# Two output projections of a hybrid trunk: keep token chunks where they first land instead of loading them again for the forms

## The chip, the cores and the metric

The kernel runs on one core of a Trainium2 chip. The metric is the device time of one execution in microseconds, as a median of several runs. The core has five engines with instruction streams of their own: TensorE (PE, with its weight loads shown apart as PEld), VectorE (DVE), ScalarE (ACT), GpSimd (POOL) and SyncE (SP). An engine works through its instructions in order; a wait at one of them holds all behind it. SyncE issues nearly all transfers between DRAM and the on-chip memory (SBUF).

## The reference, cut to what matters

Two layers on 512 latent and 128 context tokens of width 2048, in fp32. Each layer normalizes and modulates its input, projects it, runs four kinds of mixers over the columns, concatenates their gated outputs and sends them through one output projection with a gated residual:

```python
def even_mixer(h, w_in, w_out, ...):
    qa, ka, va, ga, ub, bb, cb, gb = split_cols(h @ w_in, EVEN_SPLIT)
    ...
    y_a = merge_heads(o) * jax.nn.silu(ga)
    y_b = gated_short_conv(ub, bb, cb, conv_w) * jax.nn.silu(gb)
    return jnp.concatenate([y_a, y_b], axis=-1) @ w_out, new
...
        xp = xp + gt_p * out_p
        xs = xs + gt_s * out_s
```

The odd layer's mixers are others; its last line, `jnp.concatenate([y_c, y_d], axis=-1) @ w_out`, has the same shape: (640 tokens x 2048) times (2048 x 2048). The change lies in these two products alone.

## The kernel before

The mixer's output lies in DRAM as 16 chunks `ydram[0..15]` (`yd0` to `yd15` below). Chunk k holds rows 128k to 128k + 127 of the contracted dimension, each with all 640 tokens: 128 x 640 fp32, 320 KB. fp32 products are made of three matmuls: `split` (L226 to L228) writes x as a high part (ScalarE, L227) and the rest as a low part (VectorE, L228), and `proj_q` (L263 to L265) multiplies high by high, high by low and low by high. A split chunk is `hk`, a split weight tile is `wh` and `wl`. Tokens are handled in two halves of 320 columns.

`project` computes the 16 output columns (of 128 each) in three stages:

1. `run_tiles` makes columns 0 to 2 together, over four units. A unit is a quarter of the chunks, in the order 0-3, 8-11, 4-7, 12-15; it has 3 columns x 4 chunks x 2 halves x 3 = 72 matmuls of 128x320. Before a unit, three weight tiles (`raw`, 256 KB, loaded by L240) are split, and the maker (`y0_maker`, `y1_maker`) loads and splits the unit's four chunks.
2. Column 3 alone: 96 matmuls.
3. `run_pairs`: six pairs of columns, with a Winograd-like scheme of seven products per pair. Its weights are `w8` tiles of 8 x 128 rows (A11, A21, A12; 512 KB, L519) and sums of them (L543, L546, L548). Its moving operands are halves of h and five combinations of token halves, the forms.

`forms` is a generator that makes form j from chunks j and j + 8 for j = 0 to 7, in `make_form`: three chained VectorE sums into `sx` (L1173, L1174, L1175), a difference (L1176), and the split of `sx` into T0 to T7 (ScalarE, then VectorE). The differences of forms 0 to 3 go into `room`, which lies in a tile shown as `tables`, those of 4 to 6 into `sf`, and that of form 7 over its own input. Later `project` splits the eight differences over one half of h0 to h7.

Every chunk is loaded twice. First for h: chunks 0 to 3 by the earlier maker (layer 0: L939; layer 1 chunks 0-3 and 8-11: L1726), the others by `late_yin` into the three `xr` buffers (L1217). Then again for the forms, into `w8` buffers (L1189), of which there are four: a form's two are loaded one form ahead. `w8` also takes the pairs' weights.

The order of the instructions on each engine is laid down when the program is built, by a scheduler that looks at which instruction is ready; the generators in `attn`, `forms` among them, are advanced once per column and unit. T4 to T7, `sf`, `xr`, `w8` and `sx` are buffers in one pool per projection (`lay_out`); T4 to T7 are each 7680 bytes wide per partition, three chunks' worth, and empty until their form is made. The residual inputs (L1207, `xr` too) and the sums into them (L1212) end each column.

Of the kernel before, what the change touches and what calls it, by code (L numbers as in the profile page):

```python
# [11 lines left out]
F32 = mybir.dt.float32  # L12
F32R = mybir.dt.float32r
# [7 lines left out]
P = 128  # L21
# [4 lines left out]
NT = NS + NP  # L26
HALF = NT // 2
# [23 lines left out]
def trunk_kernel(ctx: ExitStack, tc: tile.TileContext, I: dict, O: dict):  # L51
    nc = tc.nc
# [173 lines left out]
    def split(hi, lo, x):  # L226
        A.activation(hi, x, AF.Copy)  # L227
        V.tensor_sub(lo, x, hi)  # L228
# [24 lines left out]
    HV = ((0, slice(0, HALF)), (1, slice(HALF, NT)))  # L253
# [45 lines left out]
    prep, attn, early = [], [], []  # L299
# [17 lines left out]
    def drain(queue):  # L317
        while queue:
            advance(queue, 1)
# [598 lines left out]
    ydram = [dram.tile([P, NT], F32, name=f"yd{k}") for k in range(KT)]  # L918
# [215 lines left out]
    for i in range(4):  # L1134
        kv, h = i // 2, 2 * i
# [25 lines left out]
    room = [tables[:, i * HALF:(i + 1) * HALF] for i in range(4)]  # L1161
    W_OUT = [I["ev_w_out"][0], I["od_w_out"][0]]
    T, t1 = [], []
    HX = (1, 0)

    def big(tag, shape=(P, NT), dtype=F32, bufs=1):

        n = 6 * HALF if tag[0] == "T" else 8 * P
        return pools["cur"].tile([P, n], dtype, tag=tag, name=tag, bufs=bufs)

    def make_form(x, d, b11, b12, b21, b22, t):
        x2, x3, x4 = (x[:, i * HALF:(i + 1) * HALF] for i in range(3))
        V.tensor_sub(x3, b22, b12)  # L1173
        V.scalar_tensor_tensor(out=x2, in0=x3, scalar=-1.0, in1=b11, op0=ALU.mult, op1=ALU.subtract)  # L1174
        V.scalar_tensor_tensor(out=x4, in0=x2, scalar=-1.0, in1=b21, op0=ALU.mult, op1=ALU.subtract)  # L1175
        V.tensor_sub(d, b11, b12)  # L1176
        t = t.rearrange("p (s n) -> p s n", s=2)
        split(t[:, 0, :], t[:, 1, :], x)
        T.append(t)
        t1.append(d)  # L1180

    def forms():

        f = None

        def load(j):
            ts = [big("w8", bufs=4)[:, 0:NT] for _ in range(2)]
            for i in range(2):
                nc.sync.dma_start(ts[i], ydram[j + 8 * i])  # L1189
            return ts  # L1190

        T.clear()
        t1.clear()
        nxt = load(0)
        for j in range(8):
            (ya, yb), nxt = nxt, (load(j + 1) if j < 7 else None)
            b11, b12, b21, b22 = (t[:, HV[h][1]] for t in (ya, yb) for h in HX)
            x = big("sx")[:, 0:3 * HALF]
            if f is None:
                f = big("sf")  # L1200
            d = room[j] if j < 4 else f[:, (j - 4) * HALF:(j - 3) * HALF] if j < 7 else b11
            make_form(x, d, b11, b12, b21, b22, big(f"T{j}", dtype=F32R))
            yield

    def res_load(l, n):
# [7 lines left out]
                                   in1=xr[:, dsl], op0=ALU.mult, op1=ALU.add)  # L1213

    def late_yin(k):
        t = pools["cur"].tile([P, NT], F32, tag="xr", name="yin", bufs=3)
        nc.sync.dma_start(t, ydram[k])  # L1217
        split(*new_h(k), t)

    def half_of(k0, i):  # L1220
# [90 lines left out]
    def mid_tile(n):  # L1311
        return pools["cur"].tile([P, NT], F32, tag=n, name=n, bufs=1)

    def y0_maker(k):
        if k < 4:
            return make_y0(k)
        if k == 8:
            close("even")
            open_pool("mid")
            lay_out("T7 T6 T5 T4 sf xr w8 sx")  # L1320
            st["acc"], st["sq"] = (mid_tile(n) for n in ("acc", "sq"))
            attn.append(forms())
        late_yin(k)

    def squares(n, sl=slice(0, NT)):
# [364 lines left out]
    for n in range(1, 4):  # L1690
        h = heads[n]
        load, vgen = c_then(n)
# [5 lines left out]
    for n in range(4):  # L1698
# [3 lines left out]
        if n % 2 == 0:  # L1702
            load, vgen = v_then(P, I["cache_d_v"][0, 0, kv], (8 + kv,), O["new_d_v"][0, 0, kv], dense_then(n))
# [11 lines left out]
    def y1_maker(k):  # L1715
        if k == 4:
            drain(attn)
            close("odd")
            open_pool("fin")
            lay_out("T7 T6 xr T5 w8 sx sf T4")  # L1720
            attn.append(forms())
        if k % 8 >= 4:
            late_yin(k)
        else:
            t = pools["cur"].tile([P, 768], F32, tag="P", name="yin", bufs=P_BUFS)[:, 0:NT]
            nc.sync.dma_start(t, ydram[k])  # L1726
            split(*new_h(k), t)
# [82 lines left out]
```

## Time and profile before

| what | value |
|---|---|
| runs of before | 2281.57, 2284.30, 2286.61 us; median 2284.3 |
| profiled execution | 2283.16 us, its span 2281.4 us |
| TensorE busy | 2250.0 us (99%); weight loads 2175.0 (95%) |
| VectorE busy | 1602.0 us (70%) |
| ScalarE busy | 1087.4 us (48%) |
| output projection of layer 0 | from about 914 us, pairs from 976 us |
| output projection of layer 1 | from 2058 us, pairs from 2120 us |
| TensorE's granted clock | 1.00 in all stretches read |

A busy share is an average over stages. Successive matmuls of one kind start every 0.147 us here although each is shown with about 0.31 us, since they overlap; so a short stall need not show as idle time. In the rows, `L263 PE MATMUL pa<-h,wh` is the instruction of line 263 that reads tiles `h` and `wh` and writes `pa`; `yin<-yd` is a transfer from a chunk in DRAM into the tile `yin`; "A <- B: x, n, m" in the list of waits says that A waited for B x us in all, n times, at most m at once. In the table of stretches, a row gives the stretch, its length, then busy time and instructions of PE, PEld, DVE, ACT and POOL, the granted clock, the mean share of the 16 DMA engines that was busy, and GB/s.

### The profile page before, as it was taken

How to read it: one execution, taken by the hardware profiler on the slowest of the kernel's cores; microseconds unless marked ns; L12 is line 12 of the kernel's file. 1: busy time of each engine (PE TensorE's matmuls, PEld its weight loads, DVE VectorE, ACT ScalarE, POOL GpSimd, SP SyncE). 2: the span in 40 equal slices, each digit the busy share in tenths (PEclk: the TensorE clock that was granted, in tenths of full speed). 3: DMA queues.
4: the chain of work that ended last, by engine and by line, in shares of the span. 5: the costliest groups of instructions: out<-in, count | busy, mean ns of one | idle time of the engine just before them, and what ended most of it. 6: DMA issues, size and time to landing. Idle time of an engine off the chain costs nothing.

```text
span 2281.4 us, 41068 instructions
## 1 busy us (share of the span) xinstructions
PE 2250.0 (99%) x15941; PEld 2175.0 (95%) x15941; DVE 1602.0 (70%) x2830; ACT 1087.4 (48%) x2281; POOL 162.5 (7%) x226
## 2 busy tenths in 40 slices
PE   7999999999999999999999999999999999999999
PEld 5889999999999999999999999999999999999999
DVE  5666969779779777788697666565666655557765
ACT  5224535244352222444474444465565676754443
POOL 1001000010000000000100001111111100000101
PEclk9999999999999999999999999999999999999999
DMA  9975645655537564865453333523223212238642
GB/s 324 317 224 174 178 151 167 184 160 173 177 116 239 176 188 147 261 178 147 156 171 113 107 114 110 151 68 104 81 66 98 71 58 62 70 106 268 181 136 62
DMA packets 385395, 344.20 MB, mean 151 GB/s; under 512 B 16418, under 2 KB 342528, under 8 KB 384688
## 3 DMA queue, kind: packets, MB, share of 16 engines
q1 hardware_dynamic: 370624, 296.66, 43.7%
q0 software_dynamic: 13856, 42.76, 5.4%
q8 instruction: 125, 2.05, 0.4%
q10 hardware_dynamic: 720, 2.16, 0.3%
q14 instruction: 70, 0.57, 0.1%
HBM read 301.93 MB, written 39.59 MB: 150 GB/s over the span
## 4 chain that ended last, share of the span: by engine, by line
PE 86%; DMA 4%; issue 4%; DVE 3%; ACT 2%; POOL 0%; SPq 0%; POOLq 0%; DVEq 0%; ACTq 0%
PE pq L606 7%; PE pq L605 7%; PE pq L604 7%; PE pa L263 6%; PE pa L264 6%; PE pb L264 6%; PE pa L265 6%; PE pb L263 6%; PE pb L265 6%; PE pa L277 3%; PE pb L278 2%; PE pb L277 2%; PE pb L279 2%; PE pa L279 2%; PE pa L278 2%
## 5 line engine op out<-in xcount | busy, mean ns | idle before, releaser
L227 ACT ACTIVATE wh<-raw 128x512 fp32r<-128x512 f32 x418 | 263.5, 630 | 543.5 <-PE pb L264 384.4
L228 DVE TENSOR_TENSOR wl<-raw,wh 128x512 fp32r<-128x512 f32 x418 | 287.2, 688 | 201.8 <-ACT wh L227 193.5
L263 PE MATMUL pa<-h,wh 128*128 128x320 f32 x978 | 310.3, 318 | 4.2 <-ACT h L227 2.5
L264 PE MATMUL pa<-h,wh 128*128 128x320 f32 x978 | 304.3, 312 | 2.1 <-DVE h L228 2.1
L265 PE MATMUL pa<-h,wl 128*128 128x320 f32 x978 | 302.8, 310 | 0.0
L264 PE MATMUL pb<-h,wh 128*128 128x320 f32 x978 | 302.5, 309 | 0.0
L265 PE MATMUL pb<-h,wl 128*128 128x320 f32 x978 | 302.4, 309 | 0.0
L263 PE MATMUL pb<-h,wh 128*128 128x320 f32 x978 | 301.6, 309 | 0.7 <-ACT h L1420 0.7
L205 DVE SCALAR_TENSOR_TENSOR acc<-adaw,sT,acc 128x1024 f32<-128x1024 f32 x240 | 299.9, 1276 | 0.0
L604 PE MATMUL pq<-h,wh 128*128 128x320 f32 x672 | 208.7, 311 | 1.4 <-ACT wh L227 1.4
L606 PE MATMUL pq<-h,wl 128*128 128x320 f32 x672 | 207.9, 309 | 0.5 <-DVE wl L228 0.5
L605 PE MATMUL pq<-h,wh 128*128 128x320 f32 x672 | 207.7, 309 | 0.0
L263 PEld LDWEIGHTS pa<-h,wh 128*128 128x128 f32 x978 | 183.6, 188 | 18.1 <-issue 9.3
L264 PEld LDWEIGHTS pa<-h,wh 128*128 128x128 f32 x978 | 183.9, 188 | 8.7 <-DVE h L228 4.6
L263 PEld LDWEIGHTS pb<-h,wh 128*128 128x128 f32 x978 | 183.3, 188 | 1.4 <-ACT h L1420 0.9
L264 PEld LDWEIGHTS pb<-h,wh 128*128 128x128 f32 x978 | 183.6, 188 | 0.9 <-issue 0.8
L265 PEld LDWEIGHTS pa<-h,wl 128*128 128x128 f32 x978 | 183.7, 188 | 0.4 <-issue 0.4
L265 PEld LDWEIGHTS pb<-h,wl 128*128 128x128 f32 x978 | 183.6, 188 | 0.0
L606 PE MATMUL pq<-T,wl 128*128 128x320 f32 x504 | 155.1, 308 | 0.2 <-DVE wl L228 0.2
L604 PE MATMUL pq<-T,wh 128*128 128x320 f32 x504 | 155.1, 308 | 0.1
L605 PE MATMUL pq<-T,wh 128*128 128x320 f32 x504 | 155.2, 308 | 0.0
L277 PE MATMUL pa<-h,wh 128*128 128x320 f32 x448 | 146.5, 327 | 0.0
(482 smaller groups left out, 5410.6 us busy)
## 6 DMA issues: line engine op xcount, KB each, us to landing
adaw<-in_ada_w SPq DMA_DIRECT2D x128, 512.0 KB, 4.1
raw<-in_ev_w_in SPq DMA_DIRECT2D x176, 256.0 KB, 3.4
raw<-in_od_w_in SPq DMA_DIRECT2D x154, 256.0 KB, 2.9
ada<-in_ada_w SPq DMA_DIRECT2D x32, 1024.0 KB, 9.6
w<-in_od_w_in SPq DMA_DIRECT2D x27, 512.0 KB, 3.9
yd<-y POOLq DMA_DIRECT2D x32, 320.0 KB, 3.6
yin<-yd SPq DMA_DIRECT2D x32, 320.0 KB, 4.8
w<-yd SPq DMA_DIRECT2D x32, 320.0 KB, 4.4
```

The lines of the kernel that those rows point to most:

```text
L205: V.scalar_tensor_tensor(out=acc[c], in0=w, scalar=sT[:, kt, c:c + 1], in1=acc[c], op0=ALU.mult, op1=ALU.add)
L227: A.activation(hi, x, AF.Copy)
L228: V.tensor_sub(lo, x, hi)
L263: PE.matmul(ps, wh[:, i, :], hi[:, sl], start=(j == js[0] if alone else (pos == 0 and j == 0)), stop=False)
L264: PE.matmul(ps, wh[:, i, :], lo[:, sl], start=False, stop=False)
L265: last_mm[j % 4] = PE.matmul(ps, wl[:, i, :], hi[:, sl], start=False, stop=(j == js[1] - 1 if alone else (pos == 3 and j == 3)))
L277: PE.matmul(ps, wh[:, j, :], hi[:, sl], start=(qd == 0 and j == 0), stop=False)
L278: PE.matmul(ps, wh[:, j, :], lo[:, sl], start=False, stop=False)
L279: PE.matmul(ps, wl[:, j, :], hi[:, sl], start=False, stop=(qd == 3 and j == 3))
L604: PE.matmul(ps, wh[:, j, :], hi, start=(new and h == 0 and j == 0), stop=False, **kw)
L605: PE.matmul(ps, wh[:, j, :], lo, start=False, stop=False, **kw)
L606: PE.matmul(ps, wl[:, j, :], hi, start=False, stop=(h == 1 and j == 3), **kw)
```

## The change

A chunk that is needed for a form stays where it first lands, so that the form reads it there:

- Layer 0: chunks 8 to 11 are loaded into the four `w8` buffers and both split for h and read by forms 0 to 3; chunks 0 to 3 are still loaded by the forms, now into the `xr` buffers. Chunks 4 to 7 and 12 to 15 go into parts of T5, T6 and T7 (`LATE_AT`), whose own forms come later. 12 of the 32 loads go.
- Layer 1: chunks 4 to 7 and 12 to 15 go into T5 to T7 as well; forms 0 to 3 still load both of their chunks into `w8`. 8 of the 32 loads go.
- `forms` takes the layer, and yields until the chunk j + 8 is there. A form's T is taken only after its sums are in the program, because T6 and T7 hold inputs of forms 6 and 7. Form 7's difference goes into a `w8` buffer of its own.

The arithmetic is unchanged, and so are the numbers of instructions on TensorE, VectorE and ScalarE.

```diff
-        t = t.rearrange("p (s n) -> p s n", s=2)
+        t = (t() if callable(t) else t).rearrange("p (s n) -> p s n", s=2)
...
-    def forms():
-
-        f = None
+    ys, late_t = {}, {}
+    LATE_AT = {4: (5, 0), 12: (5, 1), 5: (6, 0), 13: (6, 1), 14: (6, 2), 6: (7, 0), 7: (7, 1), 15: (7, 2)}
+
+    def y_load(k, t):
+        nc.sync.dma_start(t, ydram[k])
+        return t
+
+    def forms(l):
 
         def load(j):
-            ts = [big("w8", bufs=4)[:, 0:NT] for _ in range(2)]
-            for i in range(2):
-                nc.sync.dma_start(ts[i], ydram[j + 8 * i])
-            return ts
+            if j > 3:
+                return None
+            if l == 0:
+                t = pools["cur"].tile([P, NT], F32, tag="xr", name="yin", bufs=3)
+                return y_load(j, t), None
+            return [y_load(j + 8 * i, big("w8", bufs=4)[:, 0:NT]) for i in range(2)]
...
         for j in range(8):
-            (ya, yb), nxt = nxt, (load(j + 1) if j < 7 else None)
-            b11, b12, b21, b22 = (t[:, HV[h][1]] for t in (ya, yb) for h in HX)
+            cur, nxt = nxt, load(j + 1)
+            while (l == 0 or j > 3) and j + 8 not in ys:
+                yield
+            ya, yb = cur or (ys[j], None)
+            b11, b12, b21, b22 = (t[:, HV[h][1]] for t in (ya, ys[j + 8] if yb is None else yb) for h in HX)
             x = big("sx")[:, 0:3 * HALF]
-            if f is None:
-                f = big("sf")
-            d = room[j] if j < 4 else f[:, (j - 4) * HALF:(j - 3) * HALF] if j < 7 else b11
-            make_form(x, d, b11, b12, b21, b22, big(f"T{j}", dtype=F32R))
+            d = room[j] if j < 4 else f[:, (j - 4) * HALF:(j - 3) * HALF] if j < 7 else big("w8", bufs=4)[:, 0:HALF]
+            make_form(x, d, b11, b12, b21, b22, lambda: big(f"T{j}", dtype=F32R))
             yield
...
     def late_yin(k):
-        t = pools["cur"].tile([P, NT], F32, tag="xr", name="yin", bufs=3)
-        nc.sync.dma_start(t, ydram[k])
+        if k in LATE_AT:
+            g, i = LATE_AT[k]
+            if g not in late_t:
+                late_t[g] = big(f"T{g}")
+            t = late_t[g][:, i * NT:(i + 1) * NT]
+        else:
+            t = big("w8", bufs=4)[:, 0:NT]
+        ys[k] = y_load(k, t)
         split(*new_h(k), t)
...
-            attn.append(forms())
+            attn.append(forms(0))
...
+            ys.clear()
+            late_t.clear()
+            attn.append(forms(1))
```

How this moves the transfers and VectorE's work is seen in three places. In the rows below, a name is followed by its buffer's number; the chunk is the one behind the arrow. The first place is SyncE's queue at the start of layer 0's projection, right behind nine weight loads (`raw`) that are the same in both kernels. Before, the loads for h (`yin`) and those for the forms (`w8`) alternate:

```order
L1217 DMA yin_10570<-yd8_157 128x640
L1217 DMA yin_10575<-yd9_158 128x640
L1217 DMA yin_10580<-yd10_159 128x640
L1189 DMA w8_10614<-yd0_149 128x640
L1189 DMA w8_10615<-yd8_157 128x640
L1217 DMA yin_10585<-yd11_160 128x640
L1189 DMA w8_10618<-yd1_150 128x640
L1189 DMA w8_10619<-yd9_158 128x640
L1217 DMA yin_10721<-yd4_153 128x640
L1189 DMA w8_10655<-yd2_151 128x640
L1189 DMA w8_10656<-yd10_159 128x640
L1217 DMA yin_10726<-yd5_154 128x640
```

In the changed kernel each chunk comes once, and `yin` are now the form's chunks 0 to 3:

```order
L1186 DMA w8_10570<-yd8_157 128x640
L1186 DMA w8_10575<-yd9_158 128x640
L1186 DMA w8_10580<-yd10_159 128x640
L1186 DMA w8_10585<-yd11_160 128x640
L1186 DMA yin_10615<-yd0_149 128x640
L1186 DMA yin_10617<-yd1_150 128x640
L1186 DMA yin_10651<-yd2_151 128x640
L1186 DMA T5_10713<-yd4_153 128x640
L1186 DMA T6_10718<-yd5_154 128x640
L1186 DMA yin_10685<-yd3_152 128x640
L1186 DMA T7_10723<-yd6_155 128x640
L1186 DMA T7_10723<-yd7_156 128x640
```

Behind chunk 8, chunk 11 moves from the 6th to the 4th place, chunk 7 from the 16th to the 12th and chunk 15 from the 27th to the 19th. The load of chunk 3 (the third row from the end) needs a free `xr` buffer, and so waits for VectorE's form 0; chunks 6, 7 and 12 to 15 stand behind it.

The second place is the same queue further on, where column 3 and the first pair are prepared. Before, the first pair's A11 and A21 (L519) come behind form 7's two chunks:

```order
L1189 DMA w8_10911<-yd7_156 128x640
L1189 DMA w8_10912<-yd15_164 128x640
L240 DMA raw_11151<-in_ev_w_out 128x4x128
L240 DMA raw_11153<-in_ev_w_out 128x4x128
L240 DMA raw_11393<-in_ev_w_out 128x4x128
L240 DMA raw_11395<-in_ev_w_out 128x4x128
L1207 DMA xr_11140<-x0d0_165 128x640
L519 DMA w8_11145<-in_ev_w_out 128x8x128
L519 DMA w8_11147<-in_ev_w_out 128x8x128
L1207 DMA xr_11203<-x0d1_166 128x640
```

In the changed kernel they come behind the weights of column 3 (`raw_10942` to `raw_10948`) and the residual inputs (L1216 there):

```order
L240 DMA raw_10942<-in_ev_w_out 128x4x128
L1216 DMA xr_10962<-x0d0_165 128x640
L240 DMA raw_10944<-in_ev_w_out 128x4x128
L1216 DMA xr_10996<-x0d0_165 128x640
L240 DMA raw_10946<-in_ev_w_out 128x4x128
L240 DMA raw_10948<-in_ev_w_out 128x4x128
L1216 DMA xr_11016<-x0d0_165 128x640
L240 DMA raw_11123<-in_ev_w_out 128x4x128
L240 DMA raw_11125<-in_ev_w_out 128x4x128
L519 DMA w8_11117<-in_ev_w_out 128x8x128
L519 DMA w8_11119<-in_ev_w_out 128x8x128
```

The pair's weights wait for `w8` buffers, which the forms 0 to 3 set free there, and no longer for forms 6 and 7.

The third place is VectorE before the first pair of layer 1. N5's weights are L543's sum. Before:

```order
L1174 SCALAR_TENSOR_TENSOR sx_24352<-sx_24352,w8_24322 128x320
L228 TENSOR_TENSOR wl_24522<-w8_24511,wh_24521 128x512
L1175 SCALAR_TENSOR_TENSOR sx_24352<-sx_24352,w8_24323 128x320
L1176 TENSOR_TENSOR w8_24322<-w8_24322 128x320
L228 TENSOR_TENSOR wl_24526<-w8_24511,wh_24525 128x512
L548 TENSOR_TENSOR sf_24571<-w8_24511,w8_24513 128x1024
L228 TENSOR_TENSOR T7_24353<-sx_24352,T7_24353 128x960
L228 TENSOR_TENSOR h7_24035<-w8_24322,h7_24035 128x320
L1212 SCALAR_TENSOR_TENSOR xr_24506<-pb_24335,hgt1_140,xr_24506 128x192
L1212 SCALAR_TENSOR_TENSOR xr_24506<-pb_24335,hgt1_140,xr_24506 128x128
L543 TENSOR_TENSOR sx_24529<-w8_24513,raw_24517 128x512
```

In the changed kernel:

```order
L228 TENSOR_TENSOR wl_24474<-w8_24463,wh_24473 128x512
L228 TENSOR_TENSOR T6_24282<-sx_24277,T6_24282 128x960
L548 TENSOR_TENSOR sf_24523<-w8_24463,w8_24465 128x1024
L1173 TENSOR_TENSOR sx_24303<-T7_24000 128x320
L228 TENSOR_TENSOR wl_24478<-w8_24463,wh_24477 128x512
L1174 SCALAR_TENSOR_TENSOR sx_24303<-sx_24303,T7_24000 128x320
L1175 SCALAR_TENSOR_TENSOR sx_24303<-sx_24303,T7_24000 128x320
L1221 SCALAR_TENSOR_TENSOR xr_24458<-pb_24286,hgt1_140,xr_24458 128x192
L1221 SCALAR_TENSOR_TENSOR xr_24458<-pb_24286,hgt1_140,xr_24458 128x128
L228 TENSOR_TENSOR T7_24309<-sx_24303,T7_24309 128x960
L543 TENSOR_TENSOR sx_24481<-w8_24465,raw_24469 128x512
```

The sum A11 + A21 (L548) now stands ahead of form 7, and the difference L1176 is gone from this place; L543 still comes behind form 7's split.

More of the change, by code (lines that the diff above doesn't have):

```diff
@@ L1180, in make_form @@
         t1.append(d)
-    def forms():
-        f = None
-        def load(j):
-            ts = [big("w8", bufs=4)[:, 0:NT] for _ in range(2)]
-            for i in range(2):
-                nc.sync.dma_start(ts[i], ydram[j + 8 * i])
-            return ts
+    ys, late_t = {}, {}
[4 more added lines that the diff above has]
+    def forms(l):
+        def load(j):
+            if j > 3:
[4 more added lines that the diff above has]
+            return [y_load(j + 8 * i, big("w8", bufs=4)[:, 0:NT]) for i in range(2)]
         T.clear()
         t1.clear()
+        f = big("sf")
         nxt = load(0)
         for j in range(8):
-            (ya, yb), nxt = nxt, (load(j + 1) if j < 7 else None)
-            b11, b12, b21, b22 = (t[:, HV[h][1]] for t in (ya, yb) for h in HX)
+            cur, nxt = nxt, load(j + 1)
[3 more added lines that the diff above has]
+            b11, b12, b21, b22 = (t[:, HV[h][1]] for t in (ya, ys[j + 8] if yb is None else yb) for h in HX)
             x = big("sx")[:, 0:3 * HALF]
-            if f is None:
-                f = big("sf")
-            d = room[j] if j < 4 else f[:, (j - 4) * HALF:(j - 3) * HALF] if j < 7 else b11
-            make_form(x, d, b11, b12, b21, b22, big(f"T{j}", dtype=F32R))
+            d = room[j] if j < 4 else f[:, (j - 4) * HALF:(j - 3) * HALF] if j < 7 else big("w8", bufs=4)[:, 0:HALF]
+            make_form(x, d, b11, b12, b21, b22, lambda: big(f"T{j}", dtype=F32R))
             yield
@@ L1720, in y1_maker @@
             lay_out("T7 T6 xr T5 w8 sx sf T4")
-            attn.append(forms())
+            ys.clear()
+            late_t.clear()
+            attn.append(forms(1))
         if k % 8 >= 4:
```

## The prediction

> **What bounds the kernel now.** I read the page first, for the engine that carries the span and the chain behind it.
>
> ```profile
> span 2281.4 us, 41068 instructions
> PE 2250.0 (99%) x15941; PEld 2175.0 (95%) x15941; DVE 1602.0 (70%) x2830; ACT 1087.4 (48%) x2281; POOL 162.5 (7%) x226
> PE 86%; DMA 4%; issue 4%; DVE 3%; ACT 2%; POOL 0%; SPq 0%; POOLq 0%; DVEq 0%; ACTq 0%
> yin<-yd SPq DMA_DIRECT2D x32, 320.0 KB, 4.8
> w<-yd SPq DMA_DIRECT2D x32, 320.0 KB, 4.4
> ```
>
> TensorE bounds the kernel, and no matmul is added or taken away. So the change is worth only time that TensorE loses in the two output projections, waiting for something that the token loads delay. The last two rows are the 64 loads of the branch outputs: 32 for the moving operand h, 32 for the forms. The change takes 20 of the second kind.
>
> Next I cut each projection at its own boundaries (first matmul of each unit), in the table of busy time by stretches. A unit is one quarter of the tokens' depth under three output columns, 72 matmuls. Layer 0, units 1 to 4, then the single fourth column, then the first 14 us of the pairs:
>
> ```profile
> core 0: us, PE busy (x) PEld busy (x) DVE busy (x) ACT busy (x) POOL busy (x), PEclk, DMA share, GB/s
> 914.29:924.85 10.56, 10.56 (x75) 10.56 (x73) 4.12 (x6) 2.96 (x5) 0.54 (x1) 1.00 0.58 177
> 924.85:937.81 12.96, 11.37 (x75) 10.62 (x73) 10.64 (x18) 7.21 (x11) 0.00 (x0) 1.00 0.84 281
> 937.81:949.22 11.41, 11.09 (x74) 10.56 (x73) 9.59 (x17) 5.93 (x10) 0.00 (x0) 1.00 0.89 274
> 949.22:962.01 12.79, 11.78 (x74) 10.50 (x73) 10.60 (x19) 5.67 (x8) 0.00 (x0) 1.00 0.96 306
> 962.01:976.17 14.16, 14.16 (x97) 14.16 (x97) 14.11 (x30) 8.57 (x16) 1.62 (x3) 1.00 0.89 275
> 976.17:990.25 14.08, 13.31 (x86) 12.32 (x85) 12.55 (x20) 6.50 (x12) 0.54 (x1) 1.00 0.85 246
> ```
>
> Unit 1 runs undisturbed in 10.56 us. Units 2, 3 and 4 take 12.96, 11.41 and 12.79: 2.40, 0.85 and 2.23 us lost. The DMA engines are 84 to 96% busy there. The same for layer 1, from unit 2 on:
>
> ```profile
> 2068.95:2082.15 13.20, 11.62 (x75) 10.61 (x73) 9.14 (x14) 6.75 (x11) 0.00 (x0) 1.00 0.73 231
> 2082.15:2092.71 10.56, 10.56 (x75) 10.56 (x73) 9.15 (x17) 5.24 (x9) 0.00 (x0) 1.00 0.95 312
> 2092.71:2104.10 11.39, 11.24 (x74) 10.56 (x73) 10.04 (x19) 4.58 (x7) 0.00 (x0) 1.00 0.99 315
> 2104.10:2119.74 15.64, 15.64 (x113) 15.62 (x112) 15.04 (x33) 9.09 (x18) 2.59 (x4) 1.00 0.92 282
> 2119.74:2134.00 14.26, 12.78 (x88) 12.23 (x87) 11.95 (x18) 7.60 (x17) 2.58 (x4) 1.00 0.85 250
> ```
>
> Losses of 2.64 (unit 2) and 0.83 (unit 4), and 14.26 - 12.23 = 2.03 after the pairs begin. I measure a loss against the weight loads (PEld), because the matmul busy column hides half: in unit 4 of layer 0 it leaves 12.79 - 11.78 = 1.01, the weight loads leave 2.29, and the length against unit 1 says 2.23. [...]
>
> What TensorE waits for there: the chain of waits of 920 to 990 us, and ScalarE's and SyncE's waits.
>
> ```profile
> 924.81 5.02 DMA yin<-yd
> 936.96 3.73 DMA yin<-yd
> 949.53 3.65 DMA yin<-yd
> 969.80 7.54 DMA w<-in_ev_w_out
> ACT h L227 <- DMA yin<-yd: 11.0, 6, 2.7
> SPq L1189 <- DVE sx L1174: 15.4, 6, 4.5
> ```
>
> The loads of h11, h7 and h15 are on the chain (landing 929.8, 940.7, 953.2), then the pair's first weights. ScalarE waits 11.0 us for token loads. SyncE stands 15.4 us in front of form loads (L1189), waiting for VectorE to free a w8 buffer, and every later load queues behind it. So both traffic and queue order make the h loads late.
>
> **The change part by part.**
>
> The stream of loads. Layer 0: 12 loads of 320 KB go. At the 306 GB/s of unit 4's row one takes 327.68 / 306 = 1.07 us, so 12.8 us of full DMA go. Counted in SyncE's order from y8, y11 was 6th and is 4th, y7 was 16th and is 12th, y15 was 27th and is 19th. That is 2.1, 4.3 and 8.6 us earlier at most: 927.7, 936.4 and 944.6.
>
> Unit 2, layer 0. The first wait there is for h9:
>
> ```profile
> 925.14 0.31 PE L265 MATMUL pa<-h,wl 128*128 128x320 f32 x1
> 926.42 0.41 PE L263 MATMUL pa<-h,wh 128*128 128x320 f32 x1 [0.97 <-ACT h L227]
> 927.28 0.41 PE L264 MATMUL pa<-h,wh 128*128 128x320 f32 x1 [0.45 <-DVE h L228]
> 927.53 0.31 PE L265 MATMUL pa<-h,wl 128*128 128x320 f32 x1
> ```
>
> Three steps of 0.147 us (10.56 / 72) take 2.39 us, so 1.95 of the 2.40 are h9's. y8, y9 and y10 keep their places behind the same nine weight loads, so this stays. The other 0.45 us is h11's, and goes: +0.45 (0 to 0.45).
>
> Unit 3: y7 by 936.4 lands before unit 3 begins (937.4 then). I take 0.75 of 0.85 (0.3 to 0.85).
>
> Unit 4: y15 has over 8 us in hand, and y12 to y14 come just before it. I take 2.1 of 2.23 (1.5 to 2.23).
>
> Start of the pairs, layer 0. The first pair's weights (A11, A21) were loaded into w8 behind the last form loads, at 969.80 by the chain. They now wait for form 3 only, and stand directly behind the fourth column's weights. The wait at the first weights' low part is
>
> ```profile
> 976.32 0.31 PE L605 MATMUL pq<-h,wh 128*128 128x320 f32 x1
> 977.12 0.42 PE L606 MATMUL pq<-h,wl 128*128 128x320 f32 x1 [0.49 <-DVE wl L228]
> ```
>
> and I take 0.6 for it (0 to 0.75: 976.32 would have been followed after 0.147).
>
> VectorE's cover. Every form keeps its instructions: three sums, the difference, and the split.
>
> ```profile
> L228 DVE TENSOR_TENSOR h<-yin,h 128x640 fp32r<-128x640 f32 x12 | 9.8, 821 | 3.7 <-ACT h L227 3.6
> L228 DVE TENSOR_TENSOR T<-sx,T 128x960 fp32r<-128x960 f32 x8 | 9.2, 1155 | 0.7 <-ACT T L227 0.5
> L1174 DVE SCALAR_TENSOR_TENSOR sx<-sx,w 128x320 f32<-128x320 f32 x8 | 3.9, 484 | 0.0
> L227 ACT ACTIVATE T<-sx 128x960 fp32r<-128x960 f32 x8 | 8.0, 1000 | 3.0 <-DVE sx L1175 3.0
> ```
>
> A form is 4 x 0.484 + 1.155 = 3.09 us of VectorE. From 924.85 to 976.17 VectorE is busy 10.64 + 9.59 + 10.60 + 14.11 = 44.94 of 51.32 us, so 6.38 are idle, and none of it in the fourth column. TensorE would come 0.45 + 0.75 + 2.1 + 0.6 = 3.9 us earlier, and VectorE must come as much earlier. Unit 2's 2.32 us of idle I count as lost (the data is not there), which leaves 4.06 for 3.9. That fits only if nearly every gap closes, so I take off 0.4 for lag (0 to 3.9). Layer 0: 3.5 us.
>
> Small things. Forms 6 and 7 now write T6 and T7 only after their difference (L1176) has read the tokens lying there: 0.48 us each before ScalarE's 1.00 us. VectorE has h splits and residual sums to do meanwhile; uncovered it is at most 1.0 us, and I count it in the lag. SyncE issues 20 fewer transfers, which no row of the chain shows as a bound (SPq 0%): nothing. The later allocation and the new w8 buffer for form 7's difference add no instruction; that buffer is free once form 3 has read it: nothing.
>
> Layer 1. Units 2's 2.64 us stay: its h9 to h11 come by L1726 before the change's part begins. In unit 4, y12 to y14 come a few places earlier, but y15 stands behind y3 and y11, which wait for form 1: +0.7 (0 to 0.83). The larger part is N5's weights, in the chain and the timeline:
>
> ```profile
> 2113.58 6.73 DMA w<-in_od_w_out
> 2120.33 1.23 DVE sf L548
> 2123.61 0.61 DVE sx L543
> ```
>
> ```profile
> 2123.20 0.31 PE L606 MATMUL pq<-h,wl 128*128 128x320 f32 x1
> 2124.93 0.41 PE L604 MATMUL pq<-h,wh 128*128 128x320 f32 x1 [1.42 <-ACT wh L227]
> ```
>
> A21's load starts only at 2113.58, when form 7 has let its w8 buffer go; VectorE stands for it, then has L548, the form's split, and only then L543, at which N5 hangs. TensorE's step from 2123.20 to 2124.93 loses 1.58, and 2.03 are lost in all. With A21 waiting for form 3 alone it lands well before. VectorE must then be 2.8 us early with 1.41 + 1.35 + 0.60 = 3.36 us idle in units 3, 4 and the column. I take 1.6 (0.5 to 2.0). Layer 1: 2.3 us.
>
> Sum: 3.5 + 2.3 = 5.8 us. The profiled execution took 2283.16 us, 1.1 below the median of 2284.3; it becomes 2277.4, and the median 2278.5.
>
> **The rivals.**
>
> A. VectorE takes the gain. In the fourth columns it is busy 14.11 of 14.16 and 15.04 of 15.64 us, so what it has not done before goes straight to the pairs' start. If its gaps in units 2 to 4 stay, about one form more (3.09 us) falls into each column: 3.5 - 3.1 and 2.3 - 3.1, about -0.4 in sum, so 2284 to 2285. For it: the columns' rows. Against: its gaps are waits for loads that now come earlier. Half of this gives 2281.5.
>
> B. Slower, by the same place. Forms 4 to 7 now take tokens that land among the h loads, and the order of the forms on VectorE slides back against h and residual work. If two forms more per layer fall into the columns, 6.2 us each against 3.5 and 2.3: +6.6, so 2291. It decides from one form more per layer (3.1 us). Against it: all forms' tokens are in SBUF by 944.6, some 17 us before the column.
>
> C. SyncE's queue keeps the waits. The load of y3 (layer 0) waits for form 0, since the small buffers are three, and y6, y7 and y12 to y15 stand behind it. SyncE's longest such wait was 4.5 us by its row. If form 0 slips by that, y7 comes at 940.9, as before, and unit 3 gains nothing; y15 comes at 949.1, still before its use. Layer 1's unit 4 loses its 0.7 too. Left: 5.8 - 1.5 = 4.3, so 2280.0.
>
> D. All that is lost around the loads goes, h9's waits with the earlier clearing of the DMA queue: 2.40 + 0.85 + 2.23 + 1.76 in layer 0 and 2.64 + 0.83 + 2.03 in layer 1 = 12.7, so 2271.6. Against: h9's load and those ahead of it are the same.
>
> **How the numbers follow.** A change of 0.2% (4.6 us) is about what a measurement tells from none: below 2279.7 is faster, above 2288.9 slower. Forecast, 4.6 to 8 us gained: 0.53. D or towards it: 0.07. Rival C 0.10 and A (whole or half) 0.20, both within 0.2% nearly always. B 0.10. Faster: 0.53 + 0.07 = 0.60. Slower: B. Same: 0.30. The range goes from 2273.5 (most of D left out) to 2285.5 (A whole, B left out); the likeliest case's own is 2276 to 2280.
>
> **What would show it.** Right: units 3 and 4 of layer 0 at 10.6 to 10.8 us, unit 2 at 12.5; layer 1's unit 2 still 13.2 and unit 4 about 10.7; the load of the first pair's A11 issued before 960; N5's wait for ScalarE's wh under 0.5; ScalarE's wait for token loads near 5 us in place of 11. Wrong: new waits of TensorE for T, wl or wh at P6 and N5 of 2 us or more (A, B), or unit 3 as long as before with SyncE standing before y3 (C).

## The result: 0.14% faster, about half of what was forecast

| | before | changed |
|---|---|---|
| median of 22 runs each | 2282.18 us (2278.55 to 2286.61) | 2279.20 us (2275.79 to 2285.45) |
| ratio, 95% interval | 1 | 0.9986 [0.998, 0.9993] |
| profiled execution, its span | 2283.16, 2281.4 us | 2278.45, 2276.6 us |

That is 3.2 us less, with an interval of 1.6 to 4.6. The gain is real, but it is under the 0.2% that I had called faster. That the predicted time, 2278.5, lies near the measured one is in part luck: the kernel before, in its larger set of runs, has a median 2.1 us lower than the one I started from. The forecast gain of 5.8 us has to be compared with 3.2.

The table of stretches of the changed kernel, cut as before: layer 0's units 2 to 4, the fourth column and the first 14 us of the pairs, then layer 1's.

```profile
925.37:937.47 12.10, 11.12 (x74) 10.60 (x73) 10.98 (x20) 6.98 (x10) 0.00 (x0) 1.00 0.87 295
937.47:948.42 10.95, 10.82 (x74) 10.56 (x73) 10.30 (x17) 6.94 (x10) 0.00 (x0) 1.00 0.84 288
948.42:958.98 10.56, 10.56 (x74) 10.56 (x73) 10.56 (x22) 4.67 (x7) 0.54 (x1) 1.00 0.57 159
958.98:973.06 14.08, 14.08 (x98) 14.08 (x97) 14.00 (x28) 8.50 (x16) 1.08 (x2) 1.00 0.87 267
973.06:987.14 14.08, 14.08 (x98) 13.95 (x96) 12.62 (x18) 7.00 (x13) 0.54 (x1) 1.00 0.59 170
...
2064.51:2078.22 13.71, 11.89 (x74) 10.64 (x73) 9.57 (x16) 6.52 (x10) 0.00 (x0) 1.00 0.84 275
2078.22:2088.78 10.56, 10.56 (x74) 10.56 (x73) 8.98 (x16) 5.69 (x8) 0.00 (x0) 1.00 0.80 265
2088.78:2100.88 12.10, 11.32 (x75) 10.61 (x74) 11.45 (x23) 4.43 (x6) 0.00 (x0) 1.00 0.93 280
2100.88:2116.52 15.64, 15.64 (x114) 15.62 (x112) 15.32 (x30) 9.24 (x19) 2.59 (x4) 1.00 0.64 189
2116.52:2130.78 14.26, 14.26 (x100) 14.04 (x99) 11.92 (x17) 8.28 (x17) 2.58 (x4) 1.00 0.72 205
```

In layer 0 units 3 and 4 run almost or wholly undisturbed (10.95 and 10.56 in place of 11.41 and 12.79), and the pairs start with the weight loads busy for 13.95 of 14.08 us, where 12.32 were busy before. In layer 1 the loss after the start of the pairs went from 2.03 us to 14.26 - 14.04 = 0.22. But unit 4 became longer: 12.10 in place of 11.39. In both kernels it waits for h15, the last chunk of the unit. SyncE's queue of the changed kernel, and its waits:

```profile
2078.51 1.14 SPq L1186 DMA_DIRECT2D w<-yd  x2
2079.71 1.37 SPq L1186 DMA_DIRECT2D T<-yd  x3
2083.00 1.32 SPq L1186 DMA_DIRECT2D w<-yd  x2
2084.42 0.38 SPq L1186 DMA_DIRECT2D T<-yd  x1
...
SPq L1186 <- DVE sx L1174: 7.1, 2, 5.2
ACT h L227 <- DMA T<-yd: 4.1, 2, 2.4
```

The first pair of loads (y2, y10) stands 5.2 us for form 0, y12 to y14 follow, the next pair (y3, y11) waits for form 1, and only then y15 is issued, at 2084.42. ScalarE then waits 2.4 us for it. Before, y15 stood behind the same pair and was issued at 2090.11. That is 7.96 us after unit 3 begins (2082.15), and in the changed kernel 6.20 us (2084.42 against 2078.22). Yet its transfer now takes longer, 5.6 us against 3.3, and h15 is not ready sooner. Its low part, before and changed, and TensorE's matmuls there:

```profile
2094.77 0.82 DVE L228 TENSOR_TENSOR h<-yin,h 128x640 fp32r<-128x640 f32 x1
2094.35 0.41 PE L263 MATMUL pa<-h,wh 128*128 128x320 f32 x1
2094.60 0.31 PE L263 MATMUL pb<-h,wh 128*128 128x320 f32 x1
...
2095.64 0.41 PE L264 MATMUL pa<-h,wh 128*128 128x320 f32 x1 [0.15 <-DVE h L228]
```

```profile
2090.80 0.82 DVE L228 TENSOR_TENSOR h<-T,h 128x640 fp32r<-128x640 f32 x1 [0.52 <-ACT h L227]
2090.82 0.42 PE L263 MATMUL pa<-h,wh 128*128 128x320 f32 x1 [0.33 <-ACT h L227]
2091.68 0.41 PE L264 MATMUL pa<-h,wh 128*128 128x320 f32 x1 [0.44 <-DVE h L228]
```

VectorE starts the low part 2.06 us into unit 4 before (2094.77 against 2092.71) and 2.02 us now (2090.80 against 2088.78), and the matmul that reads it (L264) starts 2.93 and 2.90 us in. What differs is TensorE's own order. Before, the scheduler had put five matmuls into `pb` between h15's first matmul and this one; in the changed program none stands there. So TensorE has done 15 matmuls of the unit by then before and 10 now, and 5 x 0.147 = 0.73 us is about the 0.71 by which the unit is longer.

### The profile page after: what moved, and what is told of

Same layout as the page of the kernel before. It is cut to its first block, busy times and chain, and to the rows that moved or that the text cites. A ratio compares the mean times of both kernels' runs of the same rounds, so it can differ in the third digit from the quotient of the medians.

```text
span 2276.6 us, 41019 instructions
## 1 busy us (share of the span) xinstructions
PE 2245.3 (99%) x15941; PEld 2173.6 (95%) x15941; DVE 1602.2 (70%) x2830; ACT 1087.0 (48%) x2281; POOL 162.7 (7%) x226
## 4 chain that ended last, share of the span: by engine, by line
PE 90%; DMA 4%; DVE 2%; ACT 2%; issue 2%; SPq 0%; POOL 0%; POOLq 0%; ACTq 0%; DVEq 0%
PE pq L606 7%; PE pq L605 7%; PE pq L604 7%; PE pa L263 6%; PE pa L264 6%; PE pb L264 6%; PE pb L263 6%; PE pb L265 6%; PE pa L265 6%; PE pa L277 3%; PE pb L278 3%; PE pb L279 3%; PE pb L277 3%; PE pa L279 3%; PE pa L278 3%; PE T L808 2%
## 5 line engine op out<-in xcount | busy, mean ns | idle before, releaser
L264 PE MATMUL pa<-h,wh 128*128 128x320 f32 x978 | 304.3, 312 | 2.0 <-DVE h L228 1.8
L264 PE MATMUL pb<-h,wh 128*128 128x320 f32 x978 | 302.5, 309 | 0.0
L264 PEld LDWEIGHTS pa<-h,wh 128*128 128x128 f32 x978 | 184.0, 188 | 7.8 <-issue 4.1
L264 PEld LDWEIGHTS pb<-h,wh 128*128 128x128 f32 x978 | 183.6, 188 | 0.9 <-issue 0.8
```

Source lines behind the costliest of these rows:

```text
L264: PE.matmul(ps, wh[:, i, :], lo[:, sl], start=False, stop=False)
```

## The experiments

Where a table is given, it holds what each stretch loses against its undisturbed length (10.56 us for a unit; for the pairs' start 14.26 us less the weight loads' busy time). "pairs" in layer 1 includes N5's weights.

**One layer alone.** Layer 1, or layer 0, is put back to two loads of each chunk.

```diff
-            attn.append(forms(1))
+            attn.append(forms_twice())
...
-            late_yin(k)
+            late_twice(k)
```

> Only layer 0's projection is changed; layer 1's loads its chunks twice as before. My theory (each projection gains by its own loads): layer 0 as in the changed kernel (units 2 to 4 at 12.1, 10.9 and 10.6 us, pairs from the first matmul at 14.1), layer 1 as before (13.2, 10.6, 11.4; about 1.6 us lost at N5's weights). Time about 5.3 us under before, as fast as the full change or faster by up to 0.6. Rival (the two layers act on each other, or the difference of the profiles is chance): layer 0's units lie between the two kernels'.

> Only layer 1's projection is changed. My theory: the wait at N5 goes (+2.0 us), but unit 4 again loses about 1.5 us in place of 0.83 and unit 2 about 3.1 in place of 2.6, so the net is 0.5 to 1 us, not to be told from before. Rival (unit 4's longer wait in the changed kernel was chance, as one profile can show): unit 4 at 10.6 to 11.0 us, net 2.3 us as predicted.

Layer 0 alone: 0.9986 [0.9977, 0.9995], 3.2 us less than before and not the 5.3 that I had expected, though as much as the full change. Layer 1 alone: 0.9996 [0.9988, 1.0005].

| loses, us | L0 unit 3 | unit 4 | pairs | L1 unit 2 | unit 4 | pairs |
|---|---|---|---|---|---|---|
| before | 0.85 | 2.23 | 1.76 | 2.64 | 0.83 | 2.03 |
| full change | 0.39 | 0 | 0.13 | 3.15 | 1.54 | 0.22 |
| layer 0 alone | 0.02 | 0 | 0.16 | 3.04 | 0.84 | 1.96 |
| layer 1 alone | 1.09 | 2.12 | 1.34 | 0.87 | 1.76 | 0.22 |

From unit 3 on, each layer loses within 0.5 us what it loses in the kernel whose code it has, so no sign is seen that the layers act on each other; unit 2 of layer 1 scatters more than that. And unit 4's longer wait in layer 1 is no chance: it comes with layer 1's change. (With that change alone h14's low part is late too, and TensorE waits 0.80 us for it.) What can be timed is layer 0's part; layer 1's is not to be told from nothing.

**Chunks 12 to 15 ahead.** In layer 1 their loads are issued with the first form's, into the same places.

```diff
             cur, nxt = nxt, load(j + 1)
+            if l == 1 and j == 0:
+                for k in range(12, 16):
+                    place(k)
```

> The full change, and in layer 1 the loads of chunks 12 to 15 are issued ahead of chunks 2, 10, 3 and 11, which wait for forms 0 and 1. My theory (h15 is late since its load stands behind theirs in SyncE's queue): y15 lands some 8 us earlier, unit 4 of layer 1 falls from 12.1 to 10.6 or 10.8 us, 1.3 to 1.5 us under the full change. Rival (VectorE, busy 11.45 of unit 4's 12.10 us, is what h15 waits for): unit 4 stays at 11.4 to 12.1, or the time moves into the fourth column or N5.

Measured: 0.9985 [0.9976, 0.9993], the same as the full change. Layer 1 from unit 4 on:

```profile
2088.90:2099.46 10.56, 10.56 (x75) 10.56 (x73) 8.29 (x16) 4.20 (x6) 0.00 (x0) 1.00 0.91 268
2099.46:2115.11 15.65, 15.65 (x114) 15.63 (x112) 15.65 (x32) 8.97 (x18) 2.58 (x4) 1.00 0.79 230
2115.11:2129.37 14.26, 12.98 (x89) 12.45 (x88) 11.66 (x18) 7.93 (x16) 2.57 (x4) 1.00 0.65 189
...
PE pq L604 <- ACT wh L227: 1.1, 1, 1.1
2118.58 1.29 DVE L543 TENSOR_TENSOR sx<-w,raw 128x512 f32<-128x512 f32 x2
```

Unit 4 is clean, as my theory said: with the loads ahead in SyncE's queue TensorE does not wait for h15, even in the order without the five matmuls. But 14.26 - 12.45 = 1.81 us are lost at N5 again, as the rival had allowed for. VectorE is busy in all 15.65 us of the fourth column: N5's weights (L543) start 29.7 us after unit 4 begins (2118.58 against 2088.90), in the full change 29.6 us (2118.37 against 2088.78). TensorE came earlier and VectorE did not, so the 1.5 us moved.

**N5's weights: buffer or traffic.** Forms 6 and 7 load their chunks again into w8, so that the first pair's A11 and A21 wait for form 6's buffers as before; 12 of the 20 loads stay away. (The prediction had named form 7; SyncE's wait there ends with form 6's last reading.)

```diff
-            if j > 3:
+            if j > 7 or 3 < j < 6:
                 return None
+            if j > 5:
+                return [y_load(j + 8 * i, big("w8", bufs=4)[:, 0:NT]) for i in range(2)]
...
-            d = room[j] if j < 4 else f[:, (j - 4) * HALF:(j - 3) * HALF] if j < 7 else big("w8", bufs=4)[:, 0:HALF]
+            d = room[j] if j < 4 else f[:, (j - 4) * HALF:(j - 3) * HALF] if j < 7 else b11
```

> The full change, but forms 6 and 7 of both layers load their chunks again, into w8: 8 of the 20 loads come back, behind the units' h loads, and the first pair's A11 and A21 wait for form 6's buffers again. My theory (N5's wait went because the pairs' weights no longer wait for those buffers): 1 to 2 us are lost again at N5 in layer 1 and 0.5 to 1.5 at the pairs' start in layer 0, while units 2 to 4 stay as in the changed kernel. Rival (less traffic as such): with 12 of 20 loads still gone, the pairs' start stays clean to 0.3 us.

Measured: 0.9996 [0.9987, 1.0005]. The rows are layer 0's units 3 and 4 and pairs, and layer 1's pairs:

```profile
937.82:948.37 10.55, 10.55 (x74) 10.55 (x73) 10.29 (x17) 6.17 (x9) 0.00 (x0) 1.00 1.01 350
948.37:958.93 10.56, 10.56 (x74) 10.56 (x73) 10.13 (x21) 4.86 (x7) 0.72 (x2) 1.00 0.66 200
973.01:987.27 14.26, 12.62 (x82) 11.63 (x81) 13.03 (x21) 6.36 (x12) 0.54 (x1) 1.00 0.66 192
...
2118.15:2132.41 14.26, 13.84 (x97) 13.59 (x96) 12.56 (x18) 7.88 (x17) 2.58 (x4) 1.00 0.89 275
```

Units 3 and 4 stay clean, and the pairs of layer 0 lose 2.63 us, more than before the change and than I expected; those of layer 1 lose 0.67, less than I expected. In layer 0 A11 is issued at 963.38, in the full change at 954.45, and ScalarE stands 5.26 us for it. So there the buffers are enough to bring the loss back, with less traffic than before the change. In layer 1 unit 4 lost 2.07 us, which gave VectorE that time, so 0.67 there decides little.

**The traffic without the buffers.** 20 transfers of 320 KB stand where the loads stood: each writes the high part of a split chunk from SBUF to a scratch buffer in DRAM.

```diff
+            if l == 0 or j > 3:
+                for k in ([j + 8] if j < 4 else [j, j + 8]):
+                    again(k)
             make_form(x, d, b11, b12, b21, b22, lambda: big(f"T{j}", dtype=F32R))
```

> The full change, with 20 transfers of 320 KB put in the places of the loads that went: each writes the high part of a split chunk from SBUF to a scratch buffer in DRAM, so DMA traffic is back and no w8 buffer is held. Theory 1 (traffic makes the h loads late): layer 0's units 3 and 4 lose 1 to 3 us again. Theory 2, mine (the w8 buffers held SyncE's queue, and with it the h loads): units 3 and 4 stay within 0.5 us of the full change, though the DMA engines are as busy as before; the pairs' start too.

Measured: 0.9992 [0.9983, 1.0001]. Layer 0's units 3 and 4 and pairs:

```profile
938.27:950.32 12.05, 11.28 (x72) 10.70 (x73) 11.76 (x20) 8.57 (x13) 0.00 (x0) 1.00 0.96 357
950.32:960.90 10.58, 10.58 (x74) 10.58 (x73) 9.44 (x17) 4.23 (x6) 0.00 (x0) 1.00 1.01 305
...
974.98:989.20 14.22, 13.77 (x90) 12.78 (x89) 12.96 (x19) 6.89 (x13) 0.54 (x1) 1.00 0.71 201
```

Both theories are half right. Unit 4, the largest term, stays clean with the DMA engines at 1.01, so the amount of traffic is not what it gains by; the order of the queue is left. y15 is issued by 941.5 here, some 9 us before unit 4; before the change it was issued at 949.53, 0.31 us after the unit began. Unit 3 loses 1.49 us and the pairs 1.44: these come back without the buffers. Whether by traffic or by order is not shown, because the copies are no exact stand-in: SyncE waits 7.1 us in all for ScalarE's high parts before them. In the kernel with the reloads of forms 6 and 7, unit 3 ran clean with the DMA engines at 1.01.

**Is VectorE the limit?** Five experiments add or take VectorE work. First, each difference is made twice (8 more operations of 128x320 in each projection):

```diff
-        V.tensor_sub(d, b11, b12)
+        (diff or V.tensor_sub)(d, b11, b12)
...
+    def twice(d, a, b):
+        V.tensor_sub(d, a, b)
+        V.tensor_sub(d, a, b)
```

> The full change, and VectorE makes each of the eight differences of each projection twice (3.2 to 3.9 us more VectorE per projection). My theory: VectorE is at its limit in both projections from unit 3 on; layer 0 has about 2 us of idle left in units 2 and 3 and loses 1 to 2.5 us at the pairs' start, layer 1 loses 2 to 4 us in unit 4 and at N5. Rival (VectorE has room left): no loss above 0.5 us in either.

Measured: 0.9995 [0.9986, 1.0004]. TensorE's first wait in layer 0's pairs is 2.10 us (below), in the range I gave; in layer 1 unit 4 loses 1.75 and the pairs 0.27, about as without the edit (1.54 and 0.22). The differences stand early there: in the full change seven of the eight start by 2091.54, the last at 2093.61, ahead of the fourth column.

Then the low parts of the differences for h0 to h7, which stand in the fourth column, are made twice:

```diff
                         split(*half_of(0, 1)(j), t1[j])
+                        if w is W_OUT[0] or w is W_OUT[1]:
+                            V.tensor_sub(half_of(0, 1)(j)[1], t1[j], half_of(0, 1)(j)[0])
```

> The full change, and in both projections VectorE makes the low parts of the eight differences for h0 to h7 twice (3.2 to 3.8 us more VectorE between form 3 and the pairs). My theory: in layer 1 N5's loss rises from 0.25 by 3 us or more, less what unit 4 already waits; in layer 0, where forms start a unit earlier but the fourth column is as full (14.00 of 14.08 us), the pairs' start loses 2 to 3.5 us. Rival (VectorE has room, as the doubled differences showed for earlier units): under 0.5 us in either.

Measured: 1.0004 [0.9995, 1.0014], so the gain is gone. The waits in layer 0's pairs, of the one and of the other kernel:

```profile
974.95 0.41 PE L606 MATMUL pq<-h,wl 128*128 128x320 f32 x1 [2.10 <-DVE wl L228]
```

```profile
975.68 0.50 PE L606 MATMUL pq<-h,wl 128*128 128x320 f32 x1 [2.68 <-DVE wl L228]
975.97 0.47 PE L604 MATMUL pq<-h,wh 128*128 128x320 f32 x1
...
2121.43:2135.69 14.26, 13.17 (x89) 12.49 (x88) 12.69 (x19) 7.85 (x16) 2.57 (x4) 1.00 0.72 212
```

With 8 x 0.40 = 3.2 us more, layer 0 waits 2.68 us where it waited for nothing: about 0.5 us of room is all VectorE has there. In layer 1 the pairs lose 1.77 in place of 0.22. Unit 4, which lies ahead of the doubled operations, loses 2.43 in place of 1.54 and so gives VectorE 0.89 us more. VectorE has thus under 1 us of room from form 3 on in either layer (3.2 - 0.89 - 1.55 = 0.76 in layer 1).

The other way round: the differences are given to GpSimd (with the early loads of chunks 12 to 15), and, in another kernel, the low parts in layer 1.

```diff
-            make_form(x, d, b11, b12, b21, b22, lambda: big(f"T{j}", dtype=F32R))
+            make_form(x, d, b11, b12, b21, b22, lambda: big(f"T{j}", dtype=F32R), G.tensor_sub)
```

```diff
-                        split(*half_of(0, 1)(j), t1[j])
+                        hi, lo = half_of(0, 1)(j)
+                        A.activation(hi, t1[j], AF.Copy)
+                        (G if w is W_OUT[1] else V).tensor_sub(lo, t1[j], hi)
```

> The kernel with the early loads of chunks 12 to 15 in layer 1, and the eight differences of the forms of each output projection are made by GpSimd in place of VectorE (8 x 0.48 us of VectorE less per projection). My theory (in layer 1 VectorE, busy in all 15.65 us of the fourth column, now sets when N5's weights are ready): the 1.86 us lost at the pairs' start with early loads falls to 0.5 or less, unit 4 stays at 10.56, and the kernel is 1.5 to 2 us under the full change. Rival (N5 waits for a transfer or for the chain of one form): N5's loss stays at 1.5 us or more. A third case: GpSimd is slow enough to hold w8 buffers, and the loads come late: unit 4 or N5 loses more than 2 us.

> The kernel with the early loads of chunks 12 to 15 in layer 1; besides, in layer 1 alone, GpSimd makes the low parts of the eight differences for h0 to h7 (8 x 0.40 us taken from VectorE between form 3 and N5's weights). My theory (from form 3 on VectorE works without a gap, some 24 us, until N5's weights; nothing else sets that moment): N5's loss falls from 1.86 us to 0.3 or less, unit 4 stays at 10.56, and layer 1 from unit 3 on loses under 0.5 us, against 1.8 in the full change and 2.9 before. Rival (it is the chain of form 7 through ScalarE, or GpSimd slows VectorE): N5's loss stays over 1 us. A third case: GpSimd is late with h0 to h7, and N5 or the pair's first product waits for it.

Measured: 0.9997 [0.9988, 1.0006] and 1.0006 [0.9997, 1.0015]. Both lost the gain, and neither settles the question, because VectorE's operations took longer beside GpSimd's (L1174 1049 ns in place of 484; see the last section): in the first, layer 0's unit 3 took 14.24 us; in the second, layer 1's fourth column took 17.61 in place of 15.65 and the pairs lost 14.26 - 11.00 = 3.26, at a granted clock of 0.88. In the first, N5 in layer 1 still lost 14.26 - 11.78 = 2.48 us.

So the last experiment took VectorE work out of that stretch without another engine. The sum A11 + A21 (L548) is made behind N5's weights, held there by a factor of 1 that is computed from them:

```diff
+                if not p and w_ap is W_OUT[1]:
+                    st8["one"] = small.tile([P, 1], F32, tag="one", name="one")
+                    V.tensor_scalar(out=st8["one"], in0=x[:, 7, 0:1], scalar1=0.0, scalar2=1.0, op0=ALU.mult, op1=ALU.add)
...
+                    V.scalar_tensor_tensor(out=f, in0=a("A11"), scalar=st8["one"], in1=a("A21"), op0=ALU.mult, op1=ALU.add)
```

> The kernel with the early loads of chunks 12 to 15 in layer 1; besides, the first pair's sum A11 + A21 (L548, 1.2 us of VectorE) is made behind N5's weights in place of ahead of them, by a scalar factor of 1 taken from that sum. My theory (VectorE's work without gaps, from form 3 to N5's weights, sets the pairs' start in layer 1): N5's loss falls by the 1.15 us that leave this stretch, from 1.86 to 0.5 to 0.9 us, unit 4 stays at 10.56, and layer 1 from unit 3 on loses under 1 us, against 1.5 to 1.8 in the full change. Rival (N5 waits for a transfer or for form 7's chain through ScalarE): N5's loss stays at 1.5 us or more. The time is about 1 us under the full change, which these rounds can barely tell.

Measured: 0.9978 [0.9969, 0.9988], 5.0 us under before. Layer 1 from unit 4 on, and form 7's split and L543 in the timeline:

```profile
2090.04:2100.60 10.56, 10.56 (x75) 10.56 (x73) 8.84 (x17) 4.32 (x6) 0.00 (x0) 1.00 0.98 296
2100.60:2116.24 15.64, 15.64 (x114) 15.62 (x112) 15.17 (x32) 9.32 (x19) 2.59 (x4) 1.00 0.77 221
2116.24:2130.50 14.26, 14.10 (x95) 13.31 (x94) 12.24 (x18) 7.97 (x17) 2.59 (x4) 1.00 0.60 181
...
2116.93 1.16 DVE L228 TENSOR_TENSOR T<-sx,T 128x960 fp32r<-128x960 f32 x1 [1.07 <-ACT T L227]
2118.59 1.28 DVE L543 TENSOR_TENSOR sx<-w,raw 128x512 f32<-128x512 f32 x2
```

L543 starts 28.55 us after unit 4 begins, 1.13 us sooner than the 29.68 with the sum ahead of it, and the loss falls from 1.81 to 0.95. That is about the price of the operation that was moved (L548, 1.22 us). So VectorE's work up to L543 sets N5. It is not unbroken at its end: VectorE stands 1.07 us for ScalarE's high part of form 7 here, 0.49 us with the early loads alone. So the rival's chain through ScalarE has a part in the 0.95 that are left; how large, no run shows. The point estimate is the best of all kernels, but its interval meets that of the full change, and the two were timed in different comparisons, so that it beats it is not shown.

**The same kernels again,** for the spread of one profile against another.

> The kernel before once more, for the spread of one profile against another: units 3 and 4 of layer 0, unit 4 of layer 1 and the pairs' starts within 0.3 us of the first profile; unit 2 of both layers may differ by 1 us or more, since it waits for loads issued only as the mixers end.

> The full change once more, for the spread of one profile against another: layer 0's units 3 and 4 at 10.6 to 11.0 us and its pairs clean within 0.3 us; layer 1's unit 4 again 1.3 to 2.0 us longer than 10.56; units 2 differ by up to 1 us.

Before took 2285.51 us in its second profiled execution, the full change 2279.86. In layer 0 before lost 0.92 and 2.98 us in units 3 and 4, the change nothing in either: the scatter of unit 4 is 0.75 us, more than I had expected, and far less than the difference. The pairs' starts lost 1.34 (layer 0) and 1.74 (layer 1) before, 0.09 and 0.22 in the change. In layer 1, unit 4 of before lost only 0.04 us this time, that of the change 1.30. Unit 2 of layer 1 lost 4.22 and 4.62 us.

## Why the prediction was right or wrong

| term | predicted gain, us | first profiles | second profiles |
|---|---|---|---|
| L0 unit 3 | 0.75 | 0.46 | 0.92 |
| L0 unit 4 | 2.1 | 2.23 | 2.98 |
| L0 pairs' start | 0.6 | 1.63 | 1.25 |
| L0 VectorE lag | -0.4 | 0 | 0 |
| L1 unit 4 | 0.7 | -0.71 | -1.26 |
| L1 N5 | 1.6 | 1.81 | 1.52 |
| unit 2, L0 and L1 | 0.45 and 0 | 0.86 and -0.51 | -0.06 and -0.40 |

- **Unit 3 and unit 4 of layer 0: right,** in size and place. I had named both traffic and the order of the queue as what delays the h loads; the runs leave the order for unit 4 (10.58 us with the traffic put back), and for unit 3 do not tell the two apart.
- **The pairs' start of layer 0 was undersized.** I counted only the first low part's wait, 0.6 (its row allows 0.80 - 0.147 = 0.65 at most, not 0.75). The losses at P6, which I had put among the 1.76 of the rival with the largest gain, went too, because A11 and A21 come earlier and VectorE had time.
- **The lag of 0.4 did not show in layer 0.** Its cover, "fits only if nearly every gap closes", was right: of the 4.06 us counted in units 3, 4 and the column 0.73 are left (0.65, 0 and 0.08), and 3.2 us more of VectorE cost 2.68.
- **The step that failed is unit 4 of layer 1, "+0.7 (0 to 0.83)"; it became -0.71 and -1.26.** The prediction saw that "y15 stands behind y3 and y11, which wait for form 1" and counted most of the loss as gained all the same. y15 stood behind these two loads in the old order too, and h15 comes no sooner: its low part starts 2.02 us into the unit in place of 2.06, in the second profiles 1.79 in place of 1.27. The step also left out TensorE's order, which had five matmuls at this place and now has none: 0.73 us. The kernel with the early loads shows that the order of the loads makes TensorE wait here; what the matmuls' order adds is read from the traces, and no run changes it alone. The queue's part is rival C's mechanism, which I had priced for layer 1 as no gain at all, not as a loss.
- **N5: right, for a reason half right.** The wait for A21 went. (It was for form 6's buffers, not form 7's: the load starts at 2113.58, form 7's first sum at 2115.99.) What is late next is VectorE (rival A's mechanism), and in the full change its lateness is hidden behind unit 4's loss. Removing that loss alone brings it back.
- **Rival D did not come:** h9's wait stayed (0.54 and 0.44 us of idle TensorE in place of 0.97 and 0.45, and unit 2 still loses 1.54). Rival B did not come.
- **That these terms add up as forecast is luck.** From unit 3 on the forecast was 0.75 + 2.1 + 0.6 - 0.4 + 0.7 + 1.6 = 5.35; in the first profiles unit 4 of layer 1 is 1.41 below its term, and layer 0's pairs and lag together 1.43 above theirs.

The terms from unit 3 on gain 0.46 + 2.23 + 1.63 - 0.71 + 1.81 = 5.4 us in the first pair of profiles and 0.92 + 2.98 + 1.25 - 1.26 + 1.52 = 5.4 in the second, and the profiled executions differ by 4.7 and 5.65 us. The timed runs say 3.2, at most 4.6. The first pair of profiled executions shows too much: that of before lies 1.0 us above its median, that of the change 0.75 below. The granted clock, which each run lists as a mean, points to another part. Of the changed kernel's 22 runs six read 1.00 and seven 0.998 or less; of the 95 runs of before in the later comparisons it is 42 and 8. The runs that read 1.00 average 2277.0 and 2281.7 us, 4.7 apart. So the changed kernel meets a lower clock more often; what sets it off there is not shown. Unit 2 of layer 1 is one candidate: over the profiles it loses between 0.87 and 4.62 us, whatever the kernel, but no profile shows that the change makes it longer.

## What to carry to other kernels

A load that is taken away can help by where it stood in the queue (layer 0's unit 4 stayed at 10.58 us with the traffic put back): ask what it waited for, and what stood behind it. When a wait in front of the bounding engine goes, look at once at the next engine's stretch of work up to the same point; if it is full, the gain can stop there (1.81 us came back here), and moving work out of this stretch is what helps (1.22 us of it gave 0.86). Look at the bounding engine's own order too: matmuls that covered a wait may stand elsewhere in the new program (five of them here, about 0.73 us). A moved load that waits for a consumer must not stand ahead of a load that the bounding engine needs sooner (unit 4 of layer 1 lost 1.54 us so, and nothing with chunks 12 to 15 ahead).

## What the runs showed of the hardware

**VectorE took longer beside GpSimd.** In the kernel above with the differences on GpSimd, those of layer 0 fill 928.8 to 939 us there (5.3 + 3.9 + 1.1 us), and most of VectorE's operations of that stretch took 1.6 to 2.4 times as long:

```profile
L1176 POOL TENSOR_TENSOR tables<-yin 128x320 f32<-128x320 f32 x4 | 5.3, 1348 | 10.2 <-DMA yin<-yd 10.1
L228 DVE TENSOR_TENSOR h<-T,h 128x640 fp32r<-128x640 f32 x2 | 3.0, 1487 | 0.0
L1173 DVE TENSOR_TENSOR sx<-w,yin 128x320 f32<-128x320 f32 x2 | 2.3, 1168 | 0.0
L1174 DVE SCALAR_TENSOR_TENSOR sx<-sx,yin 128x320 f32<-128x320 f32 x1 | 1.0, 1049 | 0.0
```

1049 and 1168 ns in place of 484 and 482, 1487 in place of 821; besides, a form's low part (128x960) 1837 in place of 1155 and a weight tile's 1362 in place of 688. One chunk's low part kept its length (818). In the kernel with the low parts on GpSimd, L1224's sum from `Sp` took 0.35 us, as in the full change, the form's sums behind it 0.91 to 1.05 in place of 0.48, and L548 stood 3.29 us behind GpSimd and then took 1.88 in place of 1.22:

```profile
2101.31 0.35 DVE L1224 SCALAR_TENSOR_TENSOR xr<-Sp,hgt,xr 128x128 f32<-128x128 f32 x1
2102.52 1.05 DVE L1174 SCALAR_TENSOR_TENSOR sx<-sx,T 128x320 f32<-128x320 f32 x1
2107.94 1.88 DVE L548 TENSOR_TENSOR sf<-w,w 128x1024 f32<-128x1024 f32 x1 [3.29 <-POOL h L1278]
```

Why some operations were longer and others not, no run shows.

**Slow matmuls behind a wait.** In the kernel with doubled differences, 1.1 us after the wait of 2.10 us the matmuls become slow, and stay so for 3.4 us:

```profile
976.24 0.47 PE L605 MATMUL pq<-h,wh 128*128 128x320 f32 x1
976.51 0.47 PE L606 MATMUL pq<-h,wl 128*128 128x320 f32 x1
...
979.44 0.38 PE L605 MATMUL pq<-h,wh 128*128 128x320 f32 x1
979.67 0.31 PE L606 MATMUL pq<-h,wl 128*128 128x320 f32 x1
...
972.39:986.65 14.26, 12.16 (x73) 11.89 (x72) 13.02 (x21) 5.66 (x10) 0.54 (x1) 0.88 0.66 207
```

They start every 0.267 us in place of 0.147, some 12 of them, so about 1.5 us more are lost behind the wait (estimated as 12 x 0.12), and the granted clock of the stretch is 0.88. After 2.68 us the slow matmuls follow at once (rows above), and the clock is 0.88 as well. After a wait of 1.8 us, at N5 in the kernel with the differences on GpSimd, the clock read 1.00. In the first profile of before the granted clock is 1.00 in every stretch shown. The long unit 2 of layer 1 has a lower clock too in the second profiles of both kernels, before and changed:

```profile
2070.78:2085.56 14.78, 13.17 (x74) 12.15 (x73) 9.14 (x14) 6.73 (x11) 0.00 (x0) 0.88 0.68 214
```

```profile
2064.67:2079.85 15.18, 13.42 (x74) 12.18 (x73) 9.57 (x16) 6.51 (x10) 0.00 (x0) 0.89 0.78 247
```

The weight loads are busy 12.15 and 12.18 us there, against 10.61 in the first profile of before, at 1.00. So about 1.5 us of that unit's scatter go with the clock. What lowers it is not shown: the changed kernel's first profile loses 3.15 us in the same unit, in waits of 0.5 us at most, and reads 1.00.
